# Two of three MLP down products computed as seven products of halves, woven between the next group's up units

## The chip, the core and the metric

The kernel runs on one core of a Trainium2 chip. The metric is the device time of one execution in microseconds (us). Three executions of the kernel before took 953.98, 954.36 and 954.49 us; the median is 954.36 us. A core has engines that run beside each other, each through its own list of instructions in order, and wait for each other by semaphores: PE (TensorE, the matmuls, with the load of the stationary operand listed apart as PEld), DVE (VectorE), ACT (ScalarE), POOL (GpSimd) and SP (SyncE, which issues most DMAs here).

## What is computed

One layer of a decoder trunk on 512 tokens of 1024 channels: a norm, an input projection, three token mixers, their merge and an output projection with residual. Behind them stands a gated MLP with a depthwise convolution of width 3 over the tokens, again with residual, and a last norm. Only the MLP is touched here:

```python
D_MODEL = 1024; SEQ = 512; D_FF = 3 * D_MODEL; FFN_CONV = 3
...
        h2 = rms_norm(x, norm_ffn[l])
        up = causal_dwconv(h2 @ w_up[l], ffn_conv_w[l], ffn_conv_b[l])
        gate_h, val_h = jnp.split(up, 2, axis=-1)
        x = x + (jax.nn.gelu(gate_h, approximate=True) * val_h) @ w_down[l]
    return rms_norm(x, final_norm)
```

w_up is 1024 x 6144, w_down 3072 x 1024, everything in float32.

## The kernel before, in words

**Products in three passes.** A float32 operand is split into a head `hi` (ACT copies it into a float32r tile, line 94) and the rest `lo` (DVE subtracts, line 95). A product of two float32 operands is then three matmuls into one PSUM bank: hi x hi, hi x lo, lo x hi (`mm3`, line 101). Every matmul of the MLP's main part takes a stationary tile of 128 x 128 and a moving one of 128 x 512; only the first three up units work on halves of the tokens.

**Units.** The program is a list of units (`unit`, `weave`, `emit`): a block of weights and the matmuls on it. The block of unit u + 2 (AHEAD = 2) is loaded by SP (`fetch`, line 152) and split by ACT and DVE just ahead of unit u's matmuls; raw weights, heads and rests have three buffers each.

**The MLP.** It goes over three groups g of 1024 of the 3072 hidden channels, one after the other:

- 16 up units (`up_units`), each 128 channels of w_up times all 512 tokens: 8 blocks of the contraction x 3 passes = 24 matmuls, the weights stationary and `h2h`, `h2l` (the normed input's head and rest) moving. Gate and value channels take turns. ACT and DVE read the result with the convolution (`up_evac`, lines 910 and 912). Behind every value unit come gelu (line 922), the product of gate and value (line 923), and its split into head and rest (`up_done`), one tile of 128 channels x 512 tokens.
- 8 down units (`down_units`, `token_units`): x2, the residual stream (4 tiles of tokens x 2 halves of columns), gets the group's activations times 1024 rows of w_down. A unit is 256 rows x 512 columns: 4 tiles of tokens x 2 blocks x 3 passes = 24 matmuls, the activations stationary and the weights moving. Behind four units DVE adds four PSUM banks to x2 (line 858). The third group's second half is done token tile by token tile, with the last norm behind it (`final`).

So the order on PE in the MLP is 16 up units, 8 down units, three times. PSUM banks of the large products rotate over 5 buffers (`psm`), and SBUF tiles of 128 x 512 over 53 slots (`apool`). A scheduler of the framework places the recorded instructions in each engine's list, so an engine's order can differ from that of the code in places.

Of the kernel before, what the change touches and what calls it, by code (L numbers as in the profile page):

```python
# [18 lines left out]
P = 128  # L19
# [24 lines left out]
# columns of the packed per-channel parameters  # L44
# [6 lines left out]
NB = 8  # L51


@with_exitstack
def trunk(ctx: ExitStack, tc: tile.TileContext, x, xT, mem, memT, par, wdecay, wch, wvd, wvg, wmk,
          wmv, wrg, wbr, wout, wup, wdown, gffn, gfin, out):
# [34 lines left out]
    # ---------------------------------------------------------------- helpers  # L91
    def split(hi, lo, src, eng=None):
        """src as its 12-bit head and the exact rest."""
        nc.scalar.activation(hi, src, AF.Copy)  # L94
        (eng or nc.vector).tensor_tensor(out=lo, in0=src, in1=hi.bitcast(F32), op=ALU.subtract)  # L95

    def mm3(ps, terms, first=True, last=True):
        """ps (+)= sum of lhsT.T @ rhs over (lhsT_hi, lhsT_lo, rhs_hi, rhs_lo)."""
        seq = [p for a, b, c, d in terms for p in ((a, c), (a, d))] + [(b, c) for a, b, c, d in terms]
        for i, (l, r) in enumerate(seq):  # L100
            nc.tensor.matmul(ps, lhsT=l, rhs=r, start=first and i == 0,  # L101
                             stop=last and i == len(seq) - 1)

    def rsqrt(v):
        """1 / sqrt(v) of [p, n] positive numbers: a guess from the exponent, three Newton steps."""
# [12 lines left out]
    def meansq(src, acc, width):  # L118
        """acc = sum of src^2 / width along the rows."""
# [3 lines left out]
    # ---------------------------------------------------------------- the program: a list of units, each a block  # L123
    # of weights and what the tensor engine does with it, and of steps of other work between them. A unit's
    # weights are fetched and split two units ahead of it.
    prog = []
    loads = []
    behind = {}  # loads issued behind the weights of a unit

    def unit(dram, n, fn, parts=1):  # L130
        """fn(W): W(j, m) is the [128, n/m] hi and lo part j of m of the [128, n] block."""
        prog.append((dram, n, fn, parts))

    def step(fn):
        prog.append((None, 0, fn, 0))

    def weave(units, steps, lead=0):
        """The units with the steps spread evenly behind them, from unit `lead` on."""
# [30 lines left out]
    def emit():  # L169
        units = [i for i, p in enumerate(prog) if p[0] is not None]  # L170
        ws, at = {}, 0
        for i, (dram, n, fn, parts) in enumerate(prog):
            if dram is None:
                fn()
                continue
            u = units.index(i)
            while at < len(units) and at <= u + AHEAD:
                p = prog[units[at]]
                ws[units[at]] = fetch(p[0], p[1], p[3])
                for h in behind.get(at, ()):  # L180
                    h()
                at += 1
            fn(ws.pop(i))

    # ---------------------------------------------------------------- constants
# [7 lines left out]
    # keeps the tensor engine busy, and its clock up, until the first loads are in  # L193
# [10 lines left out]
    def add_square(acc, a):  # L204
        """acc + a^2 / 1024, for the rows' mean squares"""
# [6 lines left out]
    def mean_square(acc, n):  # L212
        """[128, n] mean squares, plus eps, of n*128 rows from the sums over 1024/128 tiles of their transpose."""
# [6 lines left out]
    def row_bcast(rstd, n):  # L220
        """[128, n*128] tile whose column t*128+i holds rstd[i, t] in every partition."""
# [14 lines left out]
    def token_units(dram, n, lhs, nt, evac):  # L236
        """Units for evac(t, psum[128 tokens, n]) of activations @ a block of n columns of weights, 256 rows each."""
# [11 lines left out]
    def token_held(dram, n, lhs, nt, evac, between=None):  # L249
        """The same, one tile of tokens after the other, with all weights held."""  # L250
# [55 lines left out]
    def start():  # L306
        """The first two blocks of weights, beside the loads of x: the products run as it arrives."""
# [35 lines left out]
    # ---------------------------------------------------------------- memory: keys and values  # L343
    # the rows' 1/rms is applied to the products
# [3 lines left out]
    def mem_load(i):  # L348
        """Half i of the memory's transpose: head and rest with the norm's gain, sums of squares."""
# [50 lines left out]
    # per pair of heads: [h0 0:192 | 0 (64) | h1 0:192 | unused]  # L400
# [9 lines left out]
    def value_units(pr):  # L410
        # the split of these weights is shared with GpSimd
# [27 lines left out]
    # depthwise convolution of the recurrence  # L439
# [13 lines left out]
    def piece(ps, i):  # L453
        """The 32 channels of blocks 4-7 that sit beside 96 others in the product i of 12."""
# [596 lines left out]
```

## Time and profile before

| | |
|---|---|
| span of the profiled execution | 952.6 us |
| its own time (span, and what lies around it: 954.36 - 952.6) | 952.6 + about 1.8 us |
| three executions, median | 954.36 us |
| PE busy | 940.8 us (99%), 4522 matmuls |
| PEld busy | 798.2 us (84%) |
| DVE busy | 572.4 us (60%) |
| ACT busy | 452.8 us (48%) |
| POOL busy | 11.1 us (1%) |
| DMA | 95.95 MB, mean 101 GB/s |

The profile's page gives each engine's busy time, the span in 40 slices, and the chain of work that ended last. The trace behind it can be asked for waits, for a timeline of one engine, for the busy time of each engine in a stretch (windows), and for groups of like instructions with the mean duration of one. A matmul's duration in these tables overlaps with that of the next one, since matmuls are pipelined: how fast PE goes through them is read from their starts. Times in the trace are from the start of the span.

### The profile page before, as it was taken

How to read it: one execution, taken by the hardware profiler on the slowest of the kernel's cores; microseconds unless marked ns; L12 is line 12 of the kernel's file. 1: busy time of each engine (PE TensorE's matmuls, PEld its weight loads, DVE VectorE, ACT ScalarE, POOL GpSimd, SP SyncE). 2: the span in 40 equal slices, each digit the busy share in tenths (PEclk: the TensorE clock that was granted, in tenths of full speed). 3: DMA queues.
4: the chain of work that ended last, by engine and by line, in shares of the span. 5: the costliest groups of instructions: out<-in, count | busy, mean ns of one | idle time of the engine just before them, and what ended most of it. 6: DMA issues, size and time to landing. Idle time of an engine off the chain costs nothing.

```text
span 952.6 us, 11687 instructions
## 1 busy us (share of the span) xinstructions
PE 940.8 (99%) x4522; PEld 798.2 (84%) x4522; DVE 572.4 (60%) x1003; ACT 452.8 (48%) x682; POOL 11.1 (1%) x27
## 2 busy tenths in 40 slices
PE   8999999999999999999999999999999999999996
PEld 6899888887897789998888898888888888888885
DVE  7897754565744774485576756663456643556646
ACT  7565645684955783343334434442244432344432
POOL 0000000000000000000000000000000000000002
PEclk9999999999999999999999999999999999999998
DMA  7446212222232232222266202232232332322312
GB/s 231 152 138 193 67 57 68 80 92 78 75 117 79 77 99 84 78 94 72 67 197 224 77 23 88 89 105 95 90 109 89 97 102 90 107 93 91 131 45 88
DMA packets 30839, 95.95 MB, mean 101 GB/s; under 512 B 3568, under 2 KB 4736, under 8 KB 30784
## 3 DMA queue, kind: packets, MB, share of 16 engines
q1 hardware_dynamic: 30208, 94.16, 30.7%
q10 hardware_dynamic: 576, 1.05, 0.3%
q8 instruction: 35, 0.57, 0.2%
q14 instruction: 20, 0.16, 0.1%
HBM read 93.10 MB, written 2.10 MB: 100 GB/s over the span
## 4 chain that ended last, share of the span: by engine, by line
PE 95%; DVE 3%; DMA 0%; ACT 0%; issue 0%; SPq 0%; DVEq 0%; ACTq 0%
PE mm L101 89%; PE sm L101 3%; PE mm L328 1%; DVE wlo L95 1%; PE sm L787 1%; DMA m<-in_xT 0%; DVE r L95 0%; PE sm L789 0%; PE sm L773 0%; DVE m L296 0%; PE sm L760 0%; PE sm L895 0%; PE sm L808 0%; DVE hl L95 0%; PE sm L502 0%
## 5 line engine op out<-in xcount | busy, mean ns | idle before, releaser
L95 DVE TENSOR_TENSOR wlo<-raw,whi 128x1024 fp32r<-128x1024 f32 (+3 forms) x171 | 189.2, 1110 | 215.7 <-PE mm L101 98.6
L94 ACT ACTIVATE whi<-raw 128x1024 fp32r<-128x1024 f32 (+3 forms) x171 | 164.6, 966 | 198.1 <-PE mm L101 176.4
L101 PE MATMUL mm<-h2l,whi 128*128 128x512 f32 x360 | 140.1, 389 | 0.0
L101 PE MATMUL mm<-h2h,whi 128*128 128x512 f32 x360 | 139.9, 389 | 0.0
L101 PE MATMUL mm<-whi,r 128*128 128x512 f32 (+1 forms) x448 | 135.3, 381 | 0.0
L101 PE MATMUL mm<-hh,whi 128*128 128x512 f32 x288 | 113.9, 396 | 0.0
L101 PE MATMUL mm<-hl,whi 128*128 128x512 f32 x288 | 112.6, 391 | 0.0
L101 PE MATMUL mm<-r,whi 128*128 128x512 f32 (+1 forms) x448 | 98.3, 368 | 0.0
L101 PEld LDWEIGHTS mm<-whi,r 128*128 128x128 f32 x448 | 83.7, 188 | 15.0
L101 PEld LDWEIGHTS mm<-r,whi 128*128 128x128 f32 x448 | 77.9, 189 | 14.6 <-issue 0.8
L101 PE MATMUL mm<-h2h,wlo 128*128 128x512 f32 x360 | 88.9, 389 | 0.0
L101 PE MATMUL mm<-wlo,r 128*128 128x512 f32 (+1 forms) x224 | 85.6, 382 | 0.2 <-DVE wlo L95 0.2
L101 PEld LDWEIGHTS mm<-h2l,whi 128*128 128x128 f32 x360 | 67.6, 188 | 14.0
L101 PEld LDWEIGHTS mm<-h2h,wlo 128*128 128x128 f32 x360 | 67.6, 188 | 14.0
L101 PEld LDWEIGHTS mm<-h2h,whi 128*128 128x128 f32 x360 | 67.5, 188 | 13.9
L912 DVE SCALAR_TENSOR_TENSOR f<-mm,prm,f 128x511 f32<-128x511 f32 x96 | 71.7, 746 | 7.8 <-ACT f L910 6.1
L101 PE MATMUL mm<-hh,wlo 128*128 128x512 f32 x288 | 71.2, 389 | 0.0
L101 PEld LDWEIGHTS mm<-hh,whi 128*128 128x128 f32 x288 | 54.1, 188 | 11.6 <-issue 0.4
L101 PEld LDWEIGHTS mm<-hh,wlo 128*128 128x128 f32 x288 | 54.1, 188 | 11.2
L101 PEld LDWEIGHTS mm<-hl,whi 128*128 128x128 f32 x288 | 54.1, 188 | 10.7
L94 ACT ACTIVATE r<-f 128x512 fp32r<-128x512 f32 (+4 forms) x47 | 27.2, 589 | 65.0 <-DVE f L923 61.8
L101 PE MATMUL mm<-r,r 128*128 128x512 f32 (+1 forms) x240 | 56.8, 391 | 0.0
(191 smaller groups left out, 1208.0 us busy)
## 6 DMA issues: line engine op xcount, KB each, us to landing
raw<-in_wup SPq DMA_DIRECT2D x48, 512.0 KB, 3.5
raw<-in_wch SPq DMA_DIRECT2D x40, 512.0 KB, 3.3
raw<-in_wdown SPq DMA_DIRECT2D x24, 512.0 KB, 3.5
raw<-in_wbr SPq DMA_DIRECT2D x24, 384.0 KB, 3.1
raw<-in_wvg SPq DMA_DIRECT2D x12, 384.0 KB, 3.0
raw<-in_wout SPq DMA_DIRECT2D x8, 512.0 KB, 3.5
raw<-in_wmk SPq DMA_DIRECT2D x6, 512.0 KB, 3.4
raw<-in_wmv SPq DMA_DIRECT2D x8, 384.0 KB, 3.1
```

Source lines behind the costliest of these rows:

```text
L94: nc.scalar.activation(hi, src, AF.Copy)
L95: (eng or nc.vector).tensor_tensor(out=lo, in0=src, in1=hi.bitcast(F32), op=ALU.subtract)
L101: nc.tensor.matmul(ps, lhsT=l, rhs=r, start=first and i == 0, stop=last and i == len(seq) - 1)
L328: nc.tensor.matmul(ps[u], lhsT=a, rhs=b, start=q == 0 and i in (0, 2), stop=q == KD - 2 and i >= len(seq) - 2)
L787: nc.tensor.matmul(ps[:, j, :], lhsT=sT[h][:, t, :], rhs=vt[t][hp][:, j, :], start=True, stop=t == 0)
L912: nc.vector.scalar_tensor_tensor(out=a[:, j:], in0=ps[:, :S - j], scalar=col(C_FCW + 48 * (2 - j) + f), in1=a[:, j:], op0=ALU.mult, op1=AL ...
```

## The change

The products of groups 0 and 1 (2048 of the 3072 rows of w_down) are computed in another way; the third group's stays as it was. Tokens, rows and columns are halved: A11, A12, A21, A22 are 256 tokens x 512 hidden channels (the even blocks of 128 channels are the first half, the odd ones the second), B11 to B22 are 512 rows x 512 columns. Instead of eight products of halves, seven products of sums and differences are made (`down_fast`), each in two units of 256 rows, of 12 matmuls each. The keys a1, a2, c1, c2, b1, b2, b3 name them in their order; products with the same first letter add up in the same two banks, which are read behind each second unit. The four sums of activations per block are made by DVE (`sums`, `sum4`), the four differences of weights by DMAs that POOL issues and that add a block of w_down onto one that lies in SBUF (`add`). The host turns signs nowhere; it only lays w_down out by blocks. The unit list now holds, for each unit, work with its own lead (`made_unit`, `emit`): the weights of a half product are split 2 units ahead, adds are issued 6 or 7 ahead, plain loads 6 or 10 ahead.

The order of units becomes: 16 up units of group 0 alone; then up unit 0 of group 1, a1's first unit, up unit 1, a1's second unit, and so on through all 14 half-product units of group 0, and two up units alone; the same for group 2 with the half products of group 1; then the third group's down units.

```diff
-    def mm3(ps, terms, first=True, last=True):
+    def mm3(ps, terms, first=True, last=True, more=False):
...
     def unit(dram, n, fn, parts=1):
-        prog.append((dram, n, fn, parts))
+        w = {}
+        i = sum(1 for k, *_ in prog if k == "unit")
+
+        def ready():
+            w["w"] = fetch(dram, n, parts)
+            for h in behind.get(i, ()):
+                h()
+        prog.append(("unit", [(AHEAD, ready)], lambda: fn(w["w"])))
+
+    def made_unit(pre, fn):
+        prog.append(("unit", pre, fn))
...
     def emit():
+        units = [p for p in prog if p[0] == "unit"]
+        due = {}
+        for v, (_, pre, _) in enumerate(units):
+            for lead, fn in pre:
+                due.setdefault(max(0, v - lead), []).append((v, fn))
+        u = 0
+        for kind, _, fn in prog:
+            if kind == "unit":
+                for _, f in sorted(due.pop(u, ()), key=lambda d: d[0]):
+                    f()
+                u += 1
+            fn()
...
-    def up_done(ps, i, half, acts):
+    def up_done(ps, i, half, keep):
         uph[half] = up_evac(ps, NF * half + i)
         if half:
             a, b = uph[0], uph[1]
             nc.scalar.activation(a, a, AF.Gelu_apprx_tanh)
             nc.vector.tensor_tensor(out=a, in0=a, in1=b, op=ALU.mult)
-            r = (rslot(), rslot())
-            split(*r, a)
-            acts.append(r)
+            keep(a)
...
+    HT = S // 2
+
+    def down_fast(g, acts):
+        raw, w, a_in, a_sp, banks = {}, {}, {}, {}, {}
+
+        def src(q, p):
+            return wdown[g, int(q[1]) - 1, int(q[2]) - 1, p]
+
+        def load(q, p):
+            raw[q, p] = [fslot() for _ in range(2)]
+            for j in range(2):
+                loads.append(nc.sync.dma_start(raw[q, p][j], src(q, p)[:, j, :]))
+
+        def add(to, q, p):
+            for j in range(2):
+                nc.gpsimd.dma_start(raw[to, p][j], src(q, p)[:, j, :], accum_op=ALU.add)
+
+        def ready(key, q, p):
+            hi = wpool.tile([P, 2, S], F32R, tag="whi", name=nm("whi"))
+            lo = wpool.tile([P, 2, S], F32R, tag="wlo", name=nm("wlo"))
+            if q in ("B21", "B22"):
+                t = wpool.tile([P, 2, S], F32, tag="raw", name=nm("raw"), bufs=NRAW)
+                loads.append(nc.sync.dma_start(t, src(q, p)))
+                split(hi, lo, t)
+            else:
+                for j in range(2):
+                    split(hi[:, j, :], lo[:, j, :], raw[q, p][j])
+            w[key, p] = hi, lo
+
+        def sums(p):
...
+            for j in range(2):
+                tt(out=s1[:, j, :], in0=A[2, 1, j], in1=A[2, 2, j], op=ALU.subtract)
+                tt(out=s2[:, j, :], in0=s1[:, j, :], in1=A[1, 1, j], op=ALU.subtract)
+                tt(out=A[2, 1, j], in0=A[1, 1, j], in1=A[2, 1, j], op=ALU.subtract)
+            both = lambda r, c: [A[r, c, j] for j in range(2)]
+            a_in.update({("a1", p): both(1, 1), ("a2", p): both(1, 2), ("c1", p): s1, ("b1", p): s2,
+                         ("b2", p): both(2, 1), ("b3", p): both(2, 2)})
+
+        def sum4(p):
+            a_in["c2", p] = a_in["a1", p]
+            for j in range(2):
+                nc.vector.tensor_tensor(out=a_in["a1", p][j], in0=a_in["a2", p][j], in1=a_in["b1", p][:, j, :],
+                                        op=ALU.add)
+
+        def act_ready(key, p):
...
+
+        def put(t, c, src, op=ALU.add):
+            nc.vector.tensor_tensor(out=x2[t][c], in0=x2[t][c], in1=src, op=op)
+
+        def read(key, i, ps):
+            if key == "a1":
+                f = fslot()
+                nc.scalar.activation(f, ps, AF.Copy)
+                put(2 + i, 0, f)
+                put(i, 1, f, ALU.subtract)
+                put(2 + i, 1, f, ALU.subtract)
+            else:
+                put(*{"a2": (i, 0, ps), "c1": (2 + i, 1, ps), "c2": (i, 1, ps), "b1": (i, 1, ps, ALU.subtract),
+                      "b2": (2 + i, 1, ps, ALU.subtract), "b3": (2 + i, 0, ps)}[key])
+
+        def run(key, p):
+            (hi, lo), ws = a_sp.pop((key, p)), w.pop((key, p))
+            b = key[0]
+            for i in range(2):
+                if key[1] == "1" and p == 0:
+                    banks[b, i] = bank()
+                tk = slice(i * P, (i + 1) * P)
+                mm3(banks[b, i], [(hi[:, j, tk], lo[:, j, tk], ws[0][:, j, :], ws[1][:, j, :]) for j in range(2)],
+                    key[1] == "1" and p == 0, p == 1, key[1] != "1")
+                if p == 1:
+                    read(key, i, banks[b, i])
+
+        pre = {
+            "a1": ("B11", [(6, lambda p: load("B11", p)), (3, sums)]),
+            "a2": ("B21", []),
+            "c1": ("B11", [(6, lambda p: add("B11", "B12", p))]),
+            "c2": ("B22", [(3, sum4)]),
+            "b1": ("B11", [(6, lambda p: add("B11", "B22", p))]),
+            "b2": ("B12", [(10, lambda p: load("B12", p)), (7, lambda p: add("B12", "B22", p))]),
+            "b3": ("B11", [(6, lambda p: add("B11", "B21", p))]),
+        }
+        us = []
+        for key, (q, before) in pre.items():
+            for p in range(2):
+                us.append(([(n, lambda f=f, p=p: f(p)) for n, f in before] +
+                           [(AHEAD, lambda key=key, q=q, p=p: ready(key, q, p)),
+                            (1 if key == "a1" else 2, lambda key=key, p=p: act_ready(key, p))],
+                           lambda key=key, p=p: run(key, p)))
+        return us
...
-    for g in range(3):
-        acts = []
-        weave(up_units(g, acts, 3 if g == 0 else 0), [])
-        if g == 2:
-            step(lambda: gain_rows(gfin))
-        weave(down_units(wdown[g], acts, final if g == 2 else None), [])
+    acts = [[] for _ in range(3)]
...
+    weave(up_units(0, acts[0].append, 3), [])
+    for g in (1, 2):
+        fast = down_fast(g - 1, acts[g - 1])
+        for i, u in enumerate(up_units(g, halves if g == 2 else acts[g].append)):
+            unit(*u)
+            if i < len(fast):
+                made_unit(*fast[i])
+    step(lambda: gain_rows(gfin))
+    weave(down_units(wdown2, acts[2], final), [])
```

`act_ready` splits a half product's activations as `split` does, in pieces of 128 x 256, or of 128 x 512 for the sums s1 and s2; `halves` is the split of the third group's activations, as `up_done` had it.

How the instructions stand on three engines, before and now. In the names, `mm` is a PSUM bank of a large product, `whi` and `wlo` the head and rest of weights, `r` a head or rest of activations, `f` a float32 tile in SBUF, `raw` weights as loaded, `m` a tile of x2; `L` is the line in the kernel of that row.

PE, at the end of the up units of group 0 before: the last up unit's eight matmuls on `wlo`, and the first tile of tokens of the first down unit.

```order
L101 MATMUL mm_5660<-h2h,wlo_5581 128x512 x8
L101 MATMUL mm_5701<-whi_5621,r_5166 128x512
L101 MATMUL mm_5701<-wlo_5622,r_5166 128x512
L101 MATMUL mm_5701<-whi_5621,r_5235 128x512
L101 MATMUL mm_5701<-wlo_5622,r_5235 128x512
L101 MATMUL mm_5701<-whi_5621,r_5167 128x512
L101 MATMUL mm_5701<-whi_5621,r_5236 128x512
```

PE now, at the same product: the end of up unit 0 of group 1, the whole first unit of a1, and the start of up unit 1.

```order
L102 MATMUL mm_5699<-h2h,wlo_5602 128x512 x8
L102 MATMUL mm_5734<-whi_5642,r_5679 128x512
L102 MATMUL mm_5734<-wlo_5643,r_5679 128x512
L102 MATMUL mm_5734<-whi_5642,r_5679 128x512
L102 MATMUL mm_5734<-wlo_5643,r_5679 128x512
L102 MATMUL mm_5734<-whi_5642,r_5680 128x512 x2
L102 MATMUL mm_5741<-whi_5642,r_5679 128x512
L102 MATMUL mm_5741<-wlo_5643,r_5679 128x512
L102 MATMUL mm_5741<-whi_5642,r_5679 128x512
L102 MATMUL mm_5741<-wlo_5643,r_5679 128x512
L102 MATMUL mm_5741<-whi_5642,r_5680 128x512 x2
L102 MATMUL mm_5760<-h2h,whi_5687 128x512
```

A unit of the down product has become 12 matmuls of the same shape and operands on two banks, and stands between two up units. PE's list up to the MLP is the same as before.

DVE, behind the fourth down unit of group 0 before: splits of weights, and the four additions to x2.

```order
L95 TENSOR_TENSOR wlo_5762<-raw_5759,whi_5761 128x1024
L95 TENSOR_TENSOR wlo_5792<-raw_5789,whi_5791 128x1024
L858 TENSOR_TENSOR m_4553<-m_4553,mm_5701 128x512
L858 TENSOR_TENSOR m_4555<-m_4555,mm_5702 128x512
L858 TENSOR_TENSOR m_4557<-m_4557,mm_5703 128x512
L858 TENSOR_TENSOR m_4559<-m_4559,mm_5704 128x512
L95 TENSOR_TENSOR wlo_5826<-raw_5823,whi_5825 128x1024
```

DVE now, around the end of a1's second unit: the split of a2's weights, the reading of up unit 1, the split of a2's activations, and the six additions of a1 to x2.

```order
L96 TENSOR_TENSOR wlo_5792<-raw_5793,whi_5791 128x1024
L922 SCALAR_TENSOR_TENSOR f_5785<-mm_5760,prm,f_5785 128x511
L96 TENSOR_TENSOR r_5798<-f_5190,r_5797 128x256
L922 SCALAR_TENSOR_TENSOR f_5785<-mm_5760,prm,f_5785 128x510
L96 TENSOR_TENSOR r_5798<-f_5334,r_5797 128x256
L933 TENSOR_TENSOR f_5724<-f_5724,f_5785 128x512
L1030 TENSOR_TENSOR m_4557<-m_4557,f_5811 128x512
L1030 TENSOR_TENSOR m_4709<-m_4709,f_5811 128x512
L1030 TENSOR_TENSOR m_4713<-m_4713,f_5811 128x512
L1030 TENSOR_TENSOR m_4559<-m_4559,f_5822 128x512
L1030 TENSOR_TENSOR m_4711<-m_4711,f_5822 128x512
L1030 TENSOR_TENSOR m_4715<-m_4715,f_5822 128x512
```

DVE's work on the down product now stands among its work on the next group's up units. The additions of a1 read an SBUF copy (`f_5811`, `f_5822`), which ACT makes of a1's two banks.

POOL, whose list in the MLP before held only four multiplications of the last norm, now issues the adds. These are the last memset of the part before, and group 0's adds of c1 and b1 (`f_5488`, `f_5489` are the two pieces of B11's first 256 rows, `f_5564`, `f_5565` those of its second), and the first of b2.

```order
L772 MEMSET f_3466 128x512
L982 DMA f_5488<-in_wdown 128x512
L982 DMA f_5489<-in_wdown 128x512
L982 DMA f_5564<-in_wdown 128x512
L982 DMA f_5565<-in_wdown 128x512
L982 DMA f_5488<-in_wdown 128x512
L982 DMA f_5489<-in_wdown 128x512
L982 DMA f_5564<-in_wdown 128x512
L982 DMA f_5565<-in_wdown 128x512
L982 DMA f_6061<-in_wdown 128x512
```

Sixteen such DMAs of 256 KB stand there for each of the two groups, in one list, each behind the split that reads the same tile.

## Rows read from the trace of the kernel before

**Rows 1.** The page: engines' busy time, and PE and its granted clock in 40 slices.

```profile
PE 940.8 (99%) x4522; PEld 798.2 (84%) x4522; DVE 572.4 (60%) x1003; ACT 452.8 (48%) x682; POOL 11.1 (1%) x27
...
PE   8999999999999999999999999999999999999996
...
PEclk9999999999999999999999999999999999999998
```

**Rows 2.** The chain that ended last in order of time, its longest piece: start, length, what.

```profile
559.54 384.30 PE mm L101 x1728
```

**Rows 3.** The waits of PE over the whole span: total, times, longest (us).

```profile
PE sm L199 <- DVE warm L195: 1.1, 1, 1.1
...
PE mm L101 <- DVE wlo L95: 0.2, 1, 0.2
```

**Rows 4.** The timeline of PE: first down matmuls, first up ones behind them (start, length).

```profile
639.03 0.39 PE L101 MATMUL mm<-whi,r 128*128 128x512 f32 x1
639.26 0.39 PE L101 MATMUL mm<-wlo,r 128*128 128x512 f32 x1
...
682.55 0.39 PE L101 MATMUL mm<-h2h,whi 128*128 128x512 f32 x1
```

**Rows 5.** Windows: group 0's down units, group 1's up units, group 1's down units.

```profile
core 0: us, PE busy (x) PEld busy (x) DVE busy (x) ACT busy (x) POOL busy (x), PEclk, DMA share, GB/s
639.03:682.55 43.52, 43.52 (x193) 36.04 (x192) 17.05 (x19) 8.84 (x9) 0.00 (x0) 1.00 0.29 97
682.55:769.59 87.04, 87.04 (x385) 72.07 (x384) 51.13 (x61) 38.47 (x47) 0.00 (x0) 1.00 0.30 97
769.59:813.11 43.52, 43.52 (x193) 36.04 (x192) 17.04 (x19) 8.84 (x9) 0.00 (x0) 1.00 0.30 97
```

**Rows 6.** Groups by form from 639 us on: count, busy us, mean ns.

```profile
L101 PE MATMUL mm<-whi,r 128*128 128x512 f32 x320 | 99.0, 389 | 0.0
...
L95 DVE TENSOR_TENSOR wlo<-raw,whi 128x1024 fp32r<-128x1024 f32 x50 | 61.3, 1225 | 109.8 <-PE mm L101 62.6 <-ACT whi L94 47.2
...
L94 ACT ACTIVATE whi<-raw 128x1024 fp32r<-128x1024 f32 x49 | 51.7, 1056 | 71.7 <-PE mm L101 71.7
...
L910 ACT ACTIVATE f<-mm,prm 128x512 f32<-128x512 f32 x33 | 25.8, 781 | 19.5 <-PE mm L101 19.5
L912 DVE SCALAR_TENSOR_TENSOR f<-mm,prm,f 128x510 f32<-128x510 f32 x33 | 24.7, 748 | 1.2
...
L858 DVE TENSOR_TENSOR m<-m,mm 128x512 f32<-128x512 f32 x24 | 16.1, 685 | 16.6 <-PE mm L101 16.6
L95 DVE TENSOR_TENSOR r<-f,r 128x512 fp32r<-128x512 f32 x17 | 11.8, 693 | 11.9 <-ACT r L94 11.9
...
L94 ACT ACTIVATE r<-f 128x512 fp32r<-128x512 f32 x17 | 10.7, 632 | 46.0 <-DVE f L923 46.0
...
L95 DVE TENSOR_TENSOR r<-raw,r 128x512 fp32r<-128x512 f32 x8 | 5.2, 686 | 2.9 <-ACT r L94 2.9
```

**Rows 7.** Groups by form over the whole span: a subtraction of 256 columns.

```profile
L95 DVE TENSOR_TENSOR wlo<-raw,whi 128x256 fp32r<-128x256 f32 x8 | 3.1, 418 | 0.2 <-ACT whi L94 0.2
```

**Rows 8.** DMA issues: count, KB each, median us from issue to landing.

```profile
raw<-in_wdown SPq DMA_DIRECT2D x24, 512.0 KB, 3.5
...
m<-in_xT SPq DMA_DIRECT2D x8, 256.0 KB, 4.7
m<-in_x SPq DMA_DIRECT2D x8, 256.0 KB, 3.0
```

**Rows 9.** SP's waits from 600 us on: total, times, longest (us).

```profile
SPq L152 <- DVE wlo L95: 282.8, 57, 6.1
```

More of the change, by code (lines that the diff above doesn't have):

```diff
@@ L51 @@
 NB = 8
+HALF = D // 2
 @with_exitstack
 def trunk(ctx: ExitStack, tc: tile.TileContext, x, xT, mem, memT, par, wdecay, wch, wvd, wvg, wmk,
-          wmv, wrg, wbr, wout, wup, wdown, gffn, gfin, out):
+          wmv, wrg, wbr, wout, wup, wdown, wdown2, gffn, gfin, out):
     nc = tc.nc
@@ L101, in mm3 @@
             nc.tensor.matmul(ps, lhsT=l, rhs=r, start=first and i == 0,
-                             stop=last and i == len(seq) - 1)
+                             stop=last and i == len(seq) - 1, skip_group_check=more)
     def rsqrt(v):
@@ L130, in unit @@
     def unit(dram, n, fn, parts=1):
-        prog.append((dram, n, fn, parts))
+        w = {}
[7 more added lines that the diff above has]
+        prog.append(("unit", pre, fn))
     def step(fn):
-        prog.append((None, 0, fn, 0))
+        prog.append(("step", [], fn))
     def weave(units, steps, lead=0):
@@ L169, in emit @@
     def emit():
[L170 to L183, printed above, removed]
+        units = [p for p in prog if p[0] == "unit"]
[10 more added lines that the diff above has]
+            fn()
     HB = D // 2
@@ L923, in up_done, with up_units @@
             nc.vector.tensor_tensor(out=a, in0=a, in1=b, op=ALU.mult)
-            r = (rslot(), rslot())
-            split(*r, a)
-            acts.append(r)
-    def up_units(g, acts, early=0):
+            keep(a)
+    def up_units(g, keep, early=0):
         us = []
@@ L941, in fn @@
                             channel_major(v, KD, h2k, S // 2, S, ps)
-                            up_done(ps, 8 * g + m // 2, m % 2, acts)
+                            up_done(ps, 8 * g + m // 2, m % 2, keep)
                 us.append((wup[NF * half + i], D, fn, 2))
@@ L945, in up_units @@
                 us.append((wup[NF * half + i], D,
-                           lambda w, i=i, half=half: up_done(channel_major(w, KD, h2k), i, half, acts)))
+                           lambda w, i=i, half=half: up_done(channel_major(w, KD, h2k), i, half, keep)))
+        return us
[23 more added lines that the diff above has]
+        def sums(p):
+            A = {}
+            for j in range(2):
+                ev, od = acts[2 * (2 * p + j)], acts[2 * (2 * p + j) + 1]
+                for r in range(2):
+                    A[1 + r, 1, j], A[1 + r, 2, j] = ev[:, r * HT:(r + 1) * HT], od[:, r * HT:(r + 1) * HT]
+            s1, s2 = fslot((P, 2, HT)), fslot((P, 2, HT))
+            tt = nc.vector.tensor_tensor
+            for j in range(2):
[7 more added lines that the diff above has]
+            a_in["c2", p] = a_in["a1", p]
+            for j in range(2):
+                nc.vector.tensor_tensor(out=a_in["a1", p][j], in0=a_in["a2", p][j], in1=a_in["b1", p][:, j, :],
+                                        op=ALU.add)
+        def act_ready(key, p):
+            hi, lo = rslot((P, 2, HT)), rslot((P, 2, HT))
+            a = a_in[key, p]
+            if isinstance(a, list):
+                for j in range(2):
+                    split(hi[:, j, :], lo[:, j, :], a[j])
+            else:
+                split(hi, lo, a)
+            a_sp[key, p] = hi, lo
+        def put(t, c, src, op=ALU.add):
[7 more added lines that the diff above has]
+                put(2 + i, 1, f, ALU.subtract)
+            else:
+                put(*{"a2": (i, 0, ps), "c1": (2 + i, 1, ps), "c2": (i, 1, ps), "b1": (i, 1, ps, ALU.subtract),
[27 more added lines that the diff above has]
+                           lambda key=key, p=p: run(key, p)))
@@ L956, in final, with halves @@
         nc.scalar.dma_start(out[t * P:(t + 1) * P, HB:], xg)
-    for g in range(3):
-        acts = []
-        weave(up_units(g, acts, 3 if g == 0 else 0), [])
-        if g == 2:
-            step(lambda: gain_rows(gfin))
-        weave(down_units(wdown[g], acts, final if g == 2 else None), [])
+    acts = [[] for _ in range(3)]
+    def halves(a):
+        r = (rslot(), rslot())
+        split(*r, a)
+        acts[2].append(r)
+    weave(up_units(0, acts[0].append, 3), [])
[7 more added lines that the diff above has]
+    weave(down_units(wdown2, acts[2], final), [])
     emit()
@@ L1029, in _layouts @@
         "wout": tok(f["w_out"][0], 512), "wup": chan(f["w_up"][0]),
-        "wdown": np.stack([tok(wd[g * 1024:(g + 1) * 1024], 512) for g in range(3)]),
+        "wdown": wd[:2048].reshape(2, 2, 2, 2, P, 2, HALF).transpose(0, 3, 5, 1, 4, 2, 6),
+        "wdown2": tok(wd[2048:], HALF),
         "gffn": np.broadcast_to(f["norm_ffn"][0], (P, D)), "gfin": np.broadcast_to(f["final_norm"], (P, D)),
```

## Prediction

> **What bounds the kernel now.** I read the page first: PE is busy 99% of the span, DVE 60%, ACT 48% [rows 1]. Since matmuls overlap, a busy PE could still be a waiting one, so three more views follow. The chain of waits shows one piece on PE, 384.30 us long and with 1728 matmuls, unbroken through the whole MLP [rows 2]; its end, 943.84, lies 8.8 us ahead of the span's. PE's longest waits in the whole span are 1.1 us and 0.2 us [rows 3]. The granted clock is 1.00 in the three windows of groups 0 and 1, the level of 2.4 GHz [rows 5]. So the MLP lasts as long as PE's list takes, and nothing else is waited for.
>
> The price of a matmul is therefore the distance between starts. The first down matmul of group 0 starts at 639.03, the next at 639.26, and the first up matmul behind them at 682.55 [rows 4]. That is 43.52 us for 192, or 0.2267 us each. The 384 of the up units take 87.04 us [rows 5], 0.2267 us each again. The 0.389 us of the group [rows 6] is a latency and must not be multiplied.
>
> **Removed from PE.** A product had 8 units of 24 matmuls, 192. It now has 7 x 2 units of 12, 168: the same shape, the same kinds of operands, the same pairs on one stationary tile. That is 24 fewer for each of two products, 48 x 0.2267 = **10.88 us**. No other PE work changes. In the new order, an up unit is 24 x 0.2267 = 5.44 us, a half unit 2.72, a pair 8.16, and a woven group of 552 matmuls 125.1 us.
>
> **Added to DVE and ACT.** Per woven group, by mean durations [rows 6, 7]:
> - Splits of weights, DVE: a2 and c2 as before, 4 x 1.225; the other five products in two pieces per unit, 20 x 0.686 (nearest form: a rest of 512 columns from raw data). 18.6 us.
> - Splits of activations, DVE: 20 x 0.418 and 4 x 0.693. 11.1 us.
> - Sums of activations, DVE: 16 of 256 columns. Their form is not in the trace; taken at 0.418. 6.7 us. If they cost as 512 columns (0.685), 11.0.
> - Additions to x2: 18 x 0.685 = 12.3 us, eight of them before. The six of a1 read two SBUF tiles in place of SBUF and PSUM; the nearest row is 0.693.
>
> Together 48.8 us. In the stretch with group 2's up units DVE had 51.13 us in a window like it [rows 5], so it gets 99.9 of 125.1 us, 80%. Group 1's stretch loses eight splits of its own activations (8 x 0.693 = 5.5): 94.4 us, 75%. ACT gets, on top of 38.47, 4 x 1.056 + 20 x 0.632 + 24 x at most 0.632 + 2 x at most 0.781: some 72 of 125 us. Neither fills its stretch, so I cost this work at nothing, with PE as its cover. The cover can fail at a hand-over, so I followed DVE's list through the tightest ones.
>
> **Where the cover is thinnest.** Behind up unit 1 of a group, PE has a2's first matmul three up units and two half units after up unit 15 of the group before, 21.8 us; DVE has 28 instructions to do by then, 16.9 us by the rows. With its waits for PE and ACT counted in, DVE ends about 18 us, and about 20.1 in the second woven group, where the split of finished activations (0.693) and of an up unit's weights (1.225, behind ACT's 1.056) stand ahead. The margin is 3.7 and 1.7 us. At the hand-overs of a bank pair within a letter (c1 to c2, b1 to b2, b2 to b3) PE's next matmul into the bank stands one up unit, 5.44 us, behind the last one; DVE has the up unit's reading and the additions ahead, 3.3 to 4.0 us: margin 1.5 to 2.2. Splits of half units' weights have about 5.7 us. At a1 to a2, ACT's two copies (at most 0.781 each) stand before the same 5.44 us. All are positive, none is wide. A delay there would block PE with all its later matmuls, since its list is in order; the next thing late would be the reading of the following up unit.
>
> **The adds on POOL.** Sixteen DMAs of 256 KB per woven group add a block onto one in SBUF; no such DMA is in this trace. Lower bound: 3.5 us for 512 KB [rows 8], so 3.5 us for a half's two. Upper bound: the slowest plain 256 KB, 4.7 us [rows 8], one after the other and twice over because the destination must be read too, 18.8 us for two. A half's add is issued once the split that reads the tile is done, some 2 us ahead of PE's time for a1's first unit or later, and its first reader comes about 25 us or more behind it. But eight halves stand in one list: the last is wanted about 101.5 us after a1's first unit and the first wanted at about 30, so the queue keeps pace up to about (101.5 - 30) / 6 = 12 us for a half. I take them as hidden, nearer the 3.5 us row. More bytes (4.2 MB per woven group, 12.6 to 16.8 MB) raise the mean rate from 97 [rows 5] to about 133 GB/s, at a DMA share of 0.29 before.
>
> The Trainium skill ("DMA: Bandwidth & Descriptors", on the anatomy of a DMA from GpSimd) gives 2.0 us plus the bytes over 436e3 per us: an estimate of 2.6 us for 256 KB, 5.2 for a half, without a word on adding. By it the sum stays the same; no row here shows it.
>
> **SP.** B11 and B12 add plain loads, 6 and 10 units ahead. SP has slack: its waits for DVE's rests sum to 282.8 us, the longest 6.1 [rows 9]. A load waits behind them and lands 3.5 us later; the split of a half unit's weights has about 5 us to spare.
>
> **The sum.** The profile's own span is 952.6, 1.8 us below the median of 954.36, and PE's chain is what sets it. 952.6 - 10.88 = 941.7; plus 1.8: **943.5 us**.
>
> **The rivals.**
>
> *A, slower: the adds are too slow.* Each half's add is served after the one before, so one price decides. Up to 12 us nothing is lost. Beyond it, six spacings are too long: 14 us costs 6 x 2 = 12 us per woven group, 25 for both, 954.36 - 10.88 + 25 = 968.5 us; 18.8 us costs 41 per group, about 1025. The gain of 10.88 is gone at 6 x 2 x (12.9 - 12) = 10.9, so from 12.9 us on it is slower than before. For it: the operation has never been measured here, and it must read and write SBUF. Against it: the price must be over three times that of 3.5 [rows 8]. Chance 0.06.
>
> The Trainium skill ("SBUF — State Buffer", on who interferes with whom) gives a path to A: DMAs that GpSimd issues can be starved of descriptor generation while VectorE holds a port that both share, and VectorE would be busy 80% of the time here. The page also infers that tensor_tensor, the form of nearly all of it, takes only the read side that generation does not need. No row here shows it; I therefore leave the chance of A where the bounds put it.
>
> *B, DVE becomes what PE waits for.* Every hand-over above has 1.5 to 3.7 us left by means of single durations, and DVE's queue is in order: one wait for ACT ahead of an addition moves all behind it. Some ten places (five hand-overs per group) late by 1 us each give back 10 us: 953.5. Half of that gives 948.5. For it: rests of weights waited 47.2 us for ACT over 50 instructions [rows 6], about 0.9 each; DVE at 80%. Against it: 62.6 us of the same idling ended on PE, which means that DVE waited for PE's buffers, not PE for DVE. Chance 0.16.
>
> *C, matmuls cost their 0.389 us.* Then 48 of them are 18.7 us, 935.7 us. Against it: 192 in 43.52 us [rows 4, 5]. Chance 0.03.
>
> *D, the change does not take the 48 matmuls out*, or PE runs them at another pace, say as 24 units with a bubble of 0.4 us at every change: no gain. The order of instructions shows 12 per half unit, and the change of unit at 682.55 cost nothing [rows 4]. Chance 0.03.
>
> **How the numbers follow.** The forecast has 0.72. A measurement of this kernel can tell about 0.2% (1.9 us) from no change. Faster by more: forecast, C, and of B nearly all that stays below 952.4: 0.72 + 0.03 + 0.13 = 0.88. Same: the end of B near 953.5 and most of D, 0.05. Slower: A, and 0.01 left of these two, 0.07. The range begins 0.9 us below the forecast (the three runs differ by 0.5, and PE has waits of 0.2 to lose [rows 3]) and reaches to 948.2, the lower half of B.
>
> **What would show it.** Right: the piece on PE in the chain from about 559.5 stays unbroken, with 1680 matmuls and some 373.4 us; PE's longest wait stays near 0.2 us; windows of a woven group last 125.1 us with DVE at 75 to 80%; the adds' median from issue to landing is below 6 us. Wrong: PE waits at the first matmul into a bank whose additions DVE has not done (B); ACT or DVE waits for a POOL DMA in the split of the five added weights (A); the span between starts differs from 0.2267 us (C, D).

## The result, and the profile after

The changed kernel takes 943.48 us (943.43 to 943.51, four executions), the kernel before 954.42 us beside it. The ratio is 0.9886, with a 95% interval of 0.9874 to 0.9898. The forecast was 943.5 us, in a range of 942.6 to 948.2. On another chip the same kernel took 943.78 us (run `after_again`, below).

The page of the changed kernel: engines' busy time, and the granted clock of PE in 40 slices.

```profile
PE 930.4 (99%) x4474; PEld 790.1 (84%) x4474; DVE 610.7 (65%) x1119; ACT 476.9 (51%) x750; POOL 40.3 (4%) x59
...
PEclk9999999999999999999999999999999999999998
```

Against [rows 1], PE has 48 matmuls fewer, DVE 116 instructions more and POOL 32 more. PE stays at 99% and at its clock.

The chain that ended last, in order of time: the piece that answers to [rows 2], and the step behind it.

```profile
559.59 373.42 PE mm L102 x1680
...
933.04 0.70 DVE m L868
```

The piece was 384.30 us with 1728 matmuls and is 373.42 with 1680: 10.88 us shorter, and still unbroken. All of the 10.8 us by which the span fell (952.6 to 941.8) is this piece.

PE's waits over the whole span, as in [rows 3] (total, times, longest, us):

```profile
PE sm L209 <- DVE warm L205: 1.1, 1, 1.1
PE mm L338 <- ACT r L286: 0.5, 1, 0.5
...
PE mm L102 <- DVE wlo L96: 0.2, 1, 0.2
```

L209 is at the start of the kernel, L338 in the first projection, and L102 is `mm3`; all three waits lie ahead of 559 us, and so of the MLP. PE waits there as little as before.

The windows of the two woven groups (columns as in [rows 5]):

```profile
639.08:764.20 125.12, 125.12 (x554) 103.64 (x552) 87.75 (x138) 58.76 (x90) 14.01 (x16) 1.00 0.51 135
764.20:889.32 125.12, 125.12 (x554) 103.64 (x552) 90.09 (x138) 63.05 (x96) 12.22 (x14) 1.00 0.49 132
```

Each lasts 125.12 us for 552 matmuls, 0.2267 each, as in [rows 5]. DVE is busy 70% and 72% of it, ACT 47% and 50%. The DMA share rose from 0.30 to 0.5, and 97 GB/s to 132 to 135.

How near DVE and ACT are to being late stands in their timelines. DVE around the end of a1 in the second woven group, and PE's first matmul of a2:

```profile
782.95 1.35 DVE L96 TENSOR_TENSOR r<-f,r 128x512 fp32r<-128x512 f32 x3
784.23 3.70 DVE L1030 TENSOR_TENSOR m<-m,f 128x512 f32<-128x512 f32 x6
```

```profile
785.96 0.39 PE L102 MATMUL mm<-whi,r 128*128 128x512 f32 x1
```

The last split that a2 needs is done at 784.30, 20.1 us after the group's start at 764.20, and PE wants it at 785.96: 1.7 us to spare. The six additions of a1 come behind that and keep nobody waiting, since they read the SBUF copy.

DVE at the hand-over from c1 to c2 in both woven groups, and PE's first matmul of c2 into the same bank:

```profile
689.30 1.28 DVE L1030 TENSOR_TENSOR m<-m,mm 128x512 f32<-128x512 f32 x2
...
812.50 0.68 DVE L1030 TENSOR_TENSOR m<-m,mm 128x512 f32<-128x512 f32 x1
813.75 0.68 DVE L1030 TENSOR_TENSOR m<-m,mm 128x512 f32<-128x512 f32 x1
```

```profile
693.48 0.39 PE L102 MATMUL mm<-whi,r 128*128 128x512 f32 x1
...
818.60 0.39 PE L102 MATMUL mm<-whi,r 128*128 128x512 f32 x1
```

Both banks are read at 690.58 and 814.43, 2.9 and 4.2 us ahead of PE. At the other two hand-overs within a letter, b1 to b2 and b2 to b3, the banks are read 2.8 us ahead in the first stretch (at 723.29 and 739.61, PE at 726.12 and 742.44) and 4.1 us in the second.

The adds and the plain loads in the page's part on DMAs (count, size, median us from issue to landing; [rows 8] answer):

```profile
f<-in_wdown POOLq DMA_DIRECT2D x32, 256.0 KB, 5.0
...
f<-in_wdown SPq DMA_DIRECT2D x16, 256.0 KB, 4.2
```

### The profile page after: what moved, and what is told of

It is laid out like the page before. It is cut to its first block, busy times and chain, and to the rows that moved or that the text cites. A ratio compares the mean times of both kernels' runs of the same rounds, so it can differ in the third digit from the quotient of the medians.

```text
span 941.8 us, 11888 instructions
## 1 busy us (share of the span) xinstructions
PE 930.4 (99%) x4474; PEld 790.1 (84%) x4474; DVE 610.7 (65%) x1119; ACT 476.9 (51%) x750; POOL 40.3 (4%) x59
## 3 DMA queue, kind: packets, MB, share of 16 engines
q1 hardware_dynamic: 31360, 94.16, 29.7%
## 4 chain that ended last, share of the span: by engine, by line
PE 95%; DVE 3%; ACT 0%; DMA 0%; issue 0%; SPq 0%; ACTq 0%
PE mm L102 88%; PE sm L102 3%; PE mm L338 1%; DVE wlo L96 1%; PE sm L797 1%; DVE r L96 0%; DMA m<-in_xT 0%; PE sm L799 0%; PE sm L783 0%; DVE m L306 0%; PE sm L770 0%; PE sm L905 0%; PE sm L818 0%; DVE hl L96 0%; PE sm L512 0%
## 5 line engine op out<-in xcount | busy, mean ns | idle before, releaser
L96 DVE TENSOR_TENSOR wlo<-raw,whi 128x1024 fp32r<-128x1024 f32 (+3 forms) x163 | 179.3, 1105 | 150.6 <-PE mm L102 64.4
L95 ACT ACTIVATE whi<-raw 128x1024 fp32r<-128x1024 f32 (+3 forms) x163 | 156.5, 964 | 197.8 <-PE mm L102 169.3
L102 PE MATMUL mm<-h2l,whi 128*128 128x512 f32 x360 | 140.1, 389 | 0.0
L102 PE MATMUL mm<-h2h,whi 128*128 128x512 f32 x360 | 139.9, 389 | 0.0
L102 PE MATMUL mm<-whi,r 128*128 128x512 f32 (+1 forms) x416 | 129.6, 381 | 0.0
L102 PE MATMUL mm<-hh,whi 128*128 128x512 f32 x288 | 113.9, 395 | 0.0
L102 PE MATMUL mm<-hl,whi 128*128 128x512 f32 x288 | 112.6, 391 | 0.0
L102 PE MATMUL mm<-r,whi 128*128 128x512 f32 (+1 forms) x448 | 98.3, 368 | 0.0
L102 PEld LDWEIGHTS mm<-r,whi 128*128 128x128 f32 x448 | 77.9, 189 | 14.6 <-issue 0.8
L102 PEld LDWEIGHTS mm<-whi,r 128*128 128x128 f32 x416 | 77.7, 188 | 13.7
L102 PE MATMUL mm<-h2h,wlo 128*128 128x512 f32 x360 | 88.9, 389 | 0.0
L102 PE MATMUL mm<-wlo,r 128*128 128x512 f32 (+1 forms) x208 | 79.4, 382 | 0.2 <-DVE wlo L96 0.2
L102 PEld LDWEIGHTS mm<-h2h,wlo 128*128 128x128 f32 x360 | 67.6, 188 | 14.0
L102 PEld LDWEIGHTS mm<-h2l,whi 128*128 128x128 f32 x360 | 67.6, 188 | 14.0
L102 PEld LDWEIGHTS mm<-h2h,whi 128*128 128x128 f32 x360 | 67.5, 188 | 13.9
L922 DVE SCALAR_TENSOR_TENSOR f<-mm,prm,f 128x511 f32<-128x511 f32 x96 | 71.4, 745 | 6.7 <-ACT f L920 6.1
L102 PE MATMUL mm<-hh,wlo 128*128 128x512 f32 x288 | 71.2, 389 | 0.0
L102 PEld LDWEIGHTS mm<-hh,whi 128*128 128x128 f32 x288 | 54.2, 188 | 11.6 <-issue 0.4
L102 PEld LDWEIGHTS mm<-hh,wlo 128*128 128x128 f32 x288 | 54.1, 188 | 11.2
L102 PEld LDWEIGHTS mm<-hl,whi 128*128 128x128 f32 x288 | 54.1, 188 | 10.7
L102 PE MATMUL mm<-r,r 128*128 128x512 f32 (+1 forms) x240 | 56.8, 391 | 0.0
L920 ACT ACTIVATE f<-mm,prm 128x512 f32<-128x512 f32 x48 | 37.5, 781 | 35.5 <-PE mm L102 35.5
```

Of the source, the lines that this page charges most:

```text
L920: nc.scalar.activation(a, ps, AF.Identity, scale=col(C_FCW + 96 + f), bias=col(C_FCB + f))
L922: nc.vector.scalar_tensor_tensor(out=a[:, j:], in0=ps[:, :S - j], scalar=col(C_FCW + 48 * (2 - j) + f), in1=a[:, j:], op0=ALU.mult, op1=AL ...
```

## The experiments

The theory, called P: the MLP lasts as long as PE's matmuls at 0.2267 us each, and the added work lies beside them. The rivals are those of the prediction: B (DVE or ACT holds PE up), A (the adds do), and the doubt that a larger gain and a loss cancel.

**One product only.** Group 0's down product made of halves, group 1's as before.

```diff
-    for g in (1, 2):
-        fast = down_fast(g - 1, acts[g - 1])
...
+    fast = down_fast(0, acts[0])
+    for i, u in enumerate(up_units(1, lambda a: halves(a, 1))):
+        unit(*u)
+        if i < len(fast):
+            made_unit(*fast[i])
+    weave(down_units(wdown1, acts[1]), [])
+    weave(up_units(2, halves), [])
```

> Only group 0's down product is made of halves; group 1's stands behind its up units as in the kernel before. Theory P (PE's list alone sets the MLP's length, 0.2267 us a matmul): half of the gain, 943.5 + 24 x 0.2267 = 948.9 us, PE's unbroken piece 378.9 us with 1704 matmuls. Rival Q (the 10.9 us are a larger gain less a loss in one of the two woven groups, which happen to cancel): more than 1 us away from 948.9, down to 946.5 or up to 951.

Measured: 949.66 us (949.55 to 950.32), ratio 0.9952 (0.9938 to 0.9967). Its chain:

```profile
559.93 378.86 PE mm L102 x1704
938.81 0.70 DVE m L868
```

The piece has exactly the length of P. What the profiled execution (949.55) has above 948.9 lies outside it: the piece starts 0.34 us later than in the changed kernel, and some 0.2 us lie behind it. Each product gives its own 5.44 us, and nothing cancels.

**Sums, adds, copies and additions left out.** The splits stay.

```diff
-            for j in range(2):
-                nc.gpsimd.dma_start(raw[to, p][j], src(q, p)[:, j, :], accum_op=ALU.add)
+            pass
...
-                if p == 1:
-                    read(key, i, banks[b, i])
```

The sums in `sums` and `sum4` go as well; c1 and b1 then take A22 and A12 as they stand, in two pieces of 256 columns.

> The changed kernel's 168 matmuls and splits per product are kept; the sums of activations, the adds on POOL, the copies of a1's banks and the additions to x2 are left out for groups 0 and 1, so that the output lacks these products. Theory P (all of that lies beside PE): 943.5 us, within 0.5. Rival B (DVE or POOL holds PE up somewhere): faster by what they cost, 1 us or more, 942.5 us or below, down to 938 if each of ten places costs 0.5 us.

Measured: 943.66 us (943.36 to 943.94), ratio 0.9887 (0.9871 to 0.9904); the piece on PE is 373.42 us again. Taking this work away gains nothing, so it cost nothing. The splits, the larger part of what was added (29.7 of the prediction's 48.8 us on DVE), are not tried by this run; that they cost nothing is read from PE's unbroken piece at 0.2267 us a matmul.

**Half units not woven.**

```diff
...
+    for g in (0, 1):
+        weave(up_units(g, acts[g].append, 0 if g else 3), [])
+        for u in down_fast(g, acts[g]):
+            made_unit(*u)
+    weave(up_units(2, halves), [])
```

> The 14 half units of a product stand together behind their own group's up units instead of between the next group's; the sums of a1 are made one unit ahead in place of three, since the last activations come just before. Theory P with its cover taken away: 14 half units are 38.1 us of PE, DVE has some 41 us of work beside them (90.09 us in the woven stretch of group 2 less 51.13 of an up stretch) and no up unit lies between a bank's last matmul and its next letter's first. Each product then takes 46 to 50 us, 959 to 968 us in all, slower than before; PE waits for DVE at the first matmul into a bank and at the halves' rests. Rival W (the place of the units does not matter, only their number): 943.5 us.

Measured: 958.72 us (957.40 to 961.79), ratio 1.0051 (1.0033 to 1.0069): slower than before, and just under the low end of what was expected. Group 0's fourteen half units last from 639.07 to 684.70, 45.63 us in place of 38.08, and group 1's lose as much: 2 x 7.55 = 15.1 of the 15.2 us. PE's timeline in group 0's stretch, the matmuls behind a wait:

```profile
643.96 1.40 PE L102 MATMUL mm<-whi,r 128*128 128x512 f32 x4 [0.19 <-DVE r L96]
...
647.70 0.79 PE L102 MATMUL mm<-whi,r 128*128 128x512 f32 x1 [2.33 <-ACT f L1035]
...
662.24 0.96 PE L102 MATMUL mm<-whi,r 128*128 128x512 f32 x3 [1.81 <-ACT r L95]
```

Windows of the stretch with the second wait and the one behind it:

```profile
643.70:647.70 4.00, 1.47 (x6) 0.60 (x5) 4.00 (x11) 2.30 (x6) 0.00 (x0) 0.99 0.91 327
647.70:652.00 4.30, 4.30 (x12) 3.46 (x13) 4.30 (x9) 0.95 (x2) 3.96 (x6) 0.61 0.85 188
```

The three waits are 4.3 us as the view counts them, and 5.3 by the distances between starts. Behind the longest one the granted clock was 0.61 over 4.3 us, partly the level of 1.2 GHz, which costs some 4.3 x 0.39 = 1.7 us more. Two short stalls at 673 and 679 us cost 0.5, which makes 7.5 in all. The amount was near what P said without its cover, but the place was not: by the view PE waited for ACT, for the copies of a1's banks (L1035) and for the head of c2's activations, not for DVE's additions. DVE was busy throughout as well (4.00 of 4.00 and 4.30 of 4.30 us in the windows above), and no run separates the two, so ACT as the cause is read from the trace and not shown.

**Plain DMAs for the adds.**

```diff
-                nc.gpsimd.dma_start(raw[to, p][j], src(q, p)[:, j, :], accum_op=ALU.add)
+                nc.gpsimd.dma_start(raw[to, p][j], src(q, p)[:, j, :])
```

> The 32 DMAs on POOL overwrite the tile in place of adding to it, the rest stays, so that five of seven products use other weights. Theory P: 943.5 us, since the adds are hidden. On their price: if reading the destination counts, the median to landing falls from 5.0 us towards the 4.2 us of SP's plain 256 KB; if it is free, 5.0 us stays. Rival A (the adds are near their limit): a time below 943 us.

Measured: 944.47 us (one execution), with the same piece of 373.42 us on PE, which starts at 560.55 in place of 559.59; the MLP took the same time. The DMAs:

```profile
f<-in_wdown POOLq DMA_DIRECT2D x32, 256.0 KB, 3.2
...
f<-in_wdown SPq DMA_DIRECT2D x16, 256.0 KB, 4.2
```

Adding onto the destination costs 1.8 us of 5.0 per 256 KB. POOL is busy 28.1 us for the 32 DMAs with adding and 17.3 us for the plain ones, 0.88 and 0.54 us each.

**Each bank read more often.** 2 or 4 more readings by DVE ahead of the real one.

```diff
         def read(key, i, ps):
+            for _ in range(2):
+                nc.vector.tensor_tensor(out=junk, in0=x2[i][0], in1=ps, op=ALU.add)
```

> Ahead of the real reading of each bank of a half product, DVE reads it 2 more times into a tile that nobody uses: 28 more DVE instructions of about 0.62 us start to start per woven group (17.4 us, DVE from 90 to about 107 of 125.1 us in group 2's), and every bank comes free 1.2 to 2.5 us later. By the prediction's margins (1.5 to 2.2 us at c1 to c2, b1 to b2, b2 to b3, less behind up unit 1) some of these hand-overs are late by 0.3 to 1 us: 945 to 949 us, PE waiting for DVE L-reads at 4 to 8 places. By the additions' ends in the trace of the changed kernel (3 to 5 us ahead of the next letter's first matmul) all stays hidden: 943.5 us and an unbroken piece of 373.4.

> The same with 4 more readings: 56 DVE instructions, 34.7 us per woven group, DVE at about 122 to 125 of 125.1 us, and every bank free 2.5 to 5 us later. Theory P with the cover used up: PE waits, 950 to 965 us, both at the hand-overs and where weights' rests are late. Rival (DVE has more room than the rows say, since its instructions overlap): below 945 us.

Measured: 943.57 us with two, 946.41 us with four (one execution each). The woven groups' windows, with two and with four:

```profile
639.10:764.20 125.10, 125.10 (x553) 103.42 (x552) 104.41 (x166) 58.47 (x90) 13.39 (x16) 1.00 0.50 132
764.20:889.30 125.10, 125.10 (x553) 103.59 (x552) 105.53 (x166) 63.02 (x96) 12.77 (x15) 1.00 0.50 135
```

```profile
639.10:764.20 125.10, 125.08 (x550) 102.50 (x549) 117.53 (x188) 58.07 (x89) 12.10 (x14) 1.00 0.50 132
764.20:889.30 125.10, 124.12 (x545) 101.51 (x544) 120.56 (x194) 62.30 (x96) 13.90 (x16) 1.00 0.50 131
```

DVE at 105 of 125 us costs nothing; at 118 to 121 us it costs 2.9. So the hand-overs have more room than the 1.5 us I gave them, and rival B begins above 84% of DVE. At four readings I expected 950 us or more, with PE waiting at the hand-overs: a busy share of 94 to 96% still hides nearly all, and PE has only two waits there, 0.5 us for the head of a half unit's activations (ACT L95) and 0.4 us for the reading of an up unit's bank (DVE L922). The adds land in 4.9 us in both runs.

**Every block added two or three times.**

```diff
+            for _ in range(2):
+                for j in range(2):
+                    nc.gpsimd.dma_start(raw[to, p][j], src(q, p)[:, j, :], accum_op=ALU.add)
```

> Every block is added twice, one addition behind the other on the same tile: 64 DMAs on POOL, a half's four take about 2 x 5.9 = 11.8 us, since an addition waits for the one before it. The prediction's threshold for a half is 12 us: still hidden, 943.5 us, within 2. Rival A' (the adds' real room is much smaller than 12 us): 2 x 6 x 3 us or more on top, 980 us.

> Every block is added three times: a half's six take about 17.7 us, 5.7 above the threshold of 12. By rival A's rule 6 x 5.7 = 34 us late per woven group, 68 in all: 1010 us (980 to 1030), DVE and ACT waiting for POOL's DMAs in the splits of b1 and b3's weights. If the queue does not go one half after the other: 943.5 us still.

Measured (one execution each): 943.61 us with two, 972.37 us with three. PE's waits with three:

```profile
PE mm L102 <- ACT r L95: 15.5, 4, 5.0
PE mm L102 <- DVE m L1031: 2.5, 2, 1.5
```

Windows behind its four waits for ACT:

```profile
740.70:746.00 5.30, 5.22 (x12) 4.13 (x13) 3.53 (x6) 2.55 (x5) 3.51 (x4) 0.50 0.63 88
...
766.50:772.00 5.50, 5.43 (x17) 4.38 (x18) 5.26 (x8) 4.35 (x7) 0.00 (x0) 0.69 0.24 78
...
871.00:877.00 6.00, 5.50 (x17) 4.23 (x18) 5.29 (x10) 4.07 (x9) 0.86 (x1) 0.72 1.03 215
893.00:899.00 6.00, 5.58 (x13) 4.42 (x14) 2.49 (x5) 1.30 (x4) 0.86 (x1) 0.50 0.80 161
```

Rival A is real, and decides between two and three additions, where the prediction put it: with two, ACT has no wait for an add in its list. The path goes through ACT: it waits for the DMA at the heads of the added weights (62.8 us in all), and the heads of activations, which PE needs, stand behind in its list. Of the 28.8 us above adds_2, 18.0 are PE's waits, and 5.3 x 0.50 + 5.5 x 0.31 + 6 x 0.28 + 6 x 0.50 = 9.0 us are the lower clock behind them. By the distances between starts the waits come to 19.2, and the MLP begins 0.6 us later than in `adds_2` (560.25 against 559.68), which is the rest. The size was wrong, 68 against 29 us. In group 0's list the eight halves took from 635.6 to 764.9, 16.2 us each and not 17.7. The last was some 24 us behind the 101.5 that I had given it, while PE waited 11.9 us in that stretch: 101.5 is where the split is due, and PE stands only when its matmuls are. (Both are counted from the start of the stretch, 639.75 here. The prediction says from a1's first unit, 5.4 us later, which is a slip: in the changed kernel ACT begins the split of the last half at 740.82, 101.7 us behind 639.08.) That reading is worked out from the trace and was not tried by itself.

**A version with more of the same.** If only PE's matmuls count and DVE has room up to 105 of 125 us, more of them can go. The first 512 rows of the third group's product are made of seven half units as well, behind up units 9 to 15 of that group; the last 512 stay plain.

```diff
...
+    fast = down_fast(1, acts[1]) + down_fast(2, early, 1)
+    per = [1, 1, 2, 2, 2, 2, 2, 1, 1, 1, 1, 1, 1, 1, 1, 1]
+    for i, u in enumerate(up_units(2, halves)):
+        unit(*u)
+        for _ in range(per[i]):
+            made_unit(*fast.pop(0))
```

> The first 512 of the third group's 1024 rows are also done by seven products of halves, of one half unit each (12 matmuls), behind up units 9 to 15 of that group; to make room, group 1's half units stand two at a time behind up units 2 to 6. 12 matmuls fewer: theory P gives 943.5 - 12 x 0.2267 = 940.8 us. DVE gets some 24 us more in a woven stretch of 144 us (114 us, 79%, below the 106 of 125 us that cost nothing with two more readings), but each of the seven new half units reads its banks at once, 3.1 to 5.5 us of DVE beside 3.1 of the up unit in 8.16 us. If that is too dense (B), PE waits at the new hand-overs, 941 to 946 us.

> The changed kernel as it is, on the same chip, to stand beside the version above: 943.5 us, within 0.5.

Measured: 945.89 us (945.57 to 946.09), ratio 0.9910 (0.9893 to 0.9926), beside 943.78 us (943.59 to 944.82), ratio 0.9891, of the changed kernel: 2.1 us worse in place of 2.7 better. Its chain where PE's piece ends:

```profile
559.97 362.84 PE mm L102 x1632
922.82 0.02 issue
922.84 0.70 DVE m L868
...
926.27 0.60 DVE m L868
...
930.27 0.60 DVE m L868
```

No hand-over is late: the piece is unbroken, and PE has no wait of over 0.2 us in the MLP. But with 36 of its 1668 matmuls still to come DVE takes the chain over. A token tile of the last norm now comes every 2.7 us of PE, and the additions that open two tiles' norms stand 4.0 us apart on DVE (926.27, 930.27). The gain went into the tail.

The remedy: the plain remainder goes token tile by token tile for both halves of columns, 24 matmuls a tile as before.

```diff
+        for t in range(NT):
+            msq[t] = stat(2)
+            for c in range(2):
+                ps = bank()
+                for u in range(2):
+                    mm3(ps, [tuple(a[:, t * P:(t + 1) * P] for a in acts[2][2 * u + j]) + ws[2 * c + u](j, 2)
+                             for j in range(2)], u == 0, u == 1)
+                put_last(t, c, ps)
```

> As half_of_third, in which PE had no wait in the MLP but the last norms, now one every 2.7 us of PE instead of 5.4, became the end of the chain. Here the plain remainder (the third group's last 512 rows) goes token tile by token tile for both halves of columns, 24 matmuls a tile as before, with its four blocks of weights loaded 3 or 4 units ahead and the last norm's gains loaded at the start of the group. If the end of the norms was the only loss: 940.8 to 941.3 us, PE's piece 370.7 us unbroken. If the weights' splits (16 of 128x512 on DVE around up unit 15) come too late for the first tile: up to 4 us more, 941 to 945.

Measured: 942.60 us (942.44 to 943.66), ratio 0.9874 (0.9858 to 0.9891). PE's MLP lasts from 560.61 to 932.23, 371.6 us in place of 370.7, with a wait for the last up unit's activations (0.5 us by the distance between starts), and 9.7 us stand behind it in place of 8.8, since the last tile's addition waits for the tile before it on DVE. (This profile is of the slowest execution, 943.66 us, whose MLP starts 1.1 us later than the next run's.) The time lies where I had put late splits of weights, but what came late was an activation's head on ACT. The last run moves that wait away:

```diff
+            order = [(c, u) for u in range(2) for c in range(2)] if t == 0 else [(c, u) for c in range(2) for u in range(2)]
```

> As half_of_third_b, but the first token tile takes both halves of columns of the first 256 rows before the last 256, whose activations come out of the last up unit just before: 1.4 us more until they are needed. If the 0.9 us that PE's piece was longer than 370.7 were this wait: 941.7 us with the end of the norms as before in that version. If not: 942.6.

Measured: 941.81 us (941.56 to 942.01), ratio 0.9869 (0.9852 to 0.9885). PE's MLP is 371.05 us (559.50 to 930.55): 0.57 of the 0.9 us were the wait, and 0.35 are left. This is the fastest version, 1.7 us below the changed kernel's 943.5; the two were not run beside each other, and the intervals of their ratios overlap.

## Why the prediction was right

- **What bounds the kernel: right.** `bare` and `one_product` show PE's list alone. The price of 0.2267 us from starts [rows 4, 5] gave 10.88 us, and the piece is 10.88 us shorter. By the 0.389 of [rows 6] (rival C) it would have been 18.7.
- **DVE and ACT's work at nothing: right, with the size too large.** I gave DVE 94.4 and 99.9 us, 75 to 80%; the windows show 87.75 and 90.09, 70 and 72%. I added up durations, as I had refused to do for PE. Back to back, DVE's instructions overlap in the rows: six additions of 0.687 take 3.70 us and not 4.12, two of 0.68 take 1.28. ACT's bound of 72 us was 63.
- **The thinnest places: right behind up unit 1** in the second woven group (1.7 us, done at 20.1, both as forecast). That the numbers agree so well is in part luck: they were added up from durations that overstate DVE's load, and in the first woven group the last split is done at 17.1 us and not 18, with 4.7 us to spare and not 3.7. At the hand-overs within a letter 1.5 to 2.2 us were given and 2.8 to 4.2 are there. `reads_2` shows that some 16 us more of DVE per group cost nothing.
- **The adds as hidden: right.** 5.0 us each, and two in some 5.9 us, an estimate, since POOL issues the second 0.9 us behind the first; so a half lies between my 3.5 and 18.8, near the end that I took. `adds_2` and `adds_3` put the point where it decides between two additions a half and three, which took 16.2 us; 12 us lies in between and was not tried more closely. The loss beyond it was over-sized.
- **Rival A's path by the port: not seen.** The adds land in 5.0 us at DVE 70%, and in 4.9 us at 94 to 96% (`reads_4`). The prediction calls tensor_tensor the form of nearly all of DVE's work; in `reads_4` it is four fifths of the busy time in the second stretch, and the rest is scalar_tensor_tensor (L922, 24.6 of 120.56 us). The Trainium skill ("SBUF — State Buffer", on who interferes with whom) infers that tensor_tensor leaves descriptor generation alone; the trace agrees. The Trainium skill ("DMA: Bandwidth & Descriptors", anatomy of a DMA from GpSimd) gave an estimate of 2.6 us for 256 KB; 3.2 was measured plain and 5.0 with adding, and the measurement decides.
- **Rival B: not here**, at 0.16. It needs DVE between 106 and 118 us of 125. Unwoven, the same work does hold PE up (`no_weave`), by ACT as the view has it.

## What to carry to other kernels

Price a removed matmul by the distance between starts in a stretch without waits, and do the same for DVE: summed durations overstated its load by 8 to 11%. Fewer matmuls by sums and differences pay off as long as DVE, ACT and the adds have other matmuls to lie beside; the same half units lost 15.1 us when they stood together. What ends PE's list earlier must also leave the tail behind it as fast: `half_of_third` lost its gain there.

## What was not expected of the hardware

- A DMA that adds onto SBUF takes 5.0 us for 256 KB (4.9 to 5.4 in the other runs with one or two additions and the half units woven) where the plain one takes 3.2, and 1.6 times the time on POOL (0.88 against 0.54 us).
- A wait of PE can cost more than itself: behind waits of 2.3 to 5.0 us the granted clock was 0.50 to 0.72 over the next 4 to 6 us (0.50 is the level of 1.2 GHz), 9.0 us on top of 18.0 in `adds_3`. Behind the wait of 1.81 us in `no_weave` it stayed at 1.00 (662.30 to 666.00).
